# An encoder trunk on one core: both score matmuls of the attention over 128 rows, and the gate transposes of the mLSTM placed later in the program

## The chip, the cores and the metric

The kernel runs on one core of one Trainium2 chip. The metric is the device time of one execution in microseconds, as the median of repeated runs. A profile of one execution shows five engines: PE (TensorE: matmuls and transposes, with the loading of stationary operands as PEld), DVE (VectorE), ACT (ScalarE), POOL (GpSimd) and SP, whose queue issues the DMA transfers.

## The reference

Two layers on a sequence of 512 tokens with 1024 features. Each layer adds three normed sub-layers to the stream: a SwiGLU feed-forward, a mixer, a second SwiGLU feed-forward. The mixer projects its input once (`proj = h @ w_in`) and feeds two groups of heads:

- eight attention heads of 64 dimensions, with partial rotary on q and k, and three dilated windows whose outputs are merged by their softmax denominators. For the kernel this is one softmax over all 512 keys under a mask that holds the logarithm of how many windows contain a pair: `scores = q k^T + mask`, `out = softmax(scores) v`;
- four mLSTM heads of 128 dimensions in two directions, with input and forget gates (running sums and maxima of gate values along the sequence), whose sum is normed and gated.

Both are concatenated and sent through one output projection. All of it is in float32.

## The kernel before

**Exactness by halves.** PE multiplies in a float32 form that keeps fewer bits, so an operand is split into a high part (a rounding copy on ACT) and a low part (source minus high, on DVE, `lo` at line 114 and others), and a product is made of several matmuls into the same PSUM bank: `mm3` at lines 117 to 120 does high times high, high times low, low times high, each contracting over 128 rows.

**The scores.** A head has only 64 dimensions, so two parts fit into the 128 partitions. `stack` (lines 821 to 835) transposes the q or the k of a pair of heads (`hp`, two heads `e` = 0 and 1) into one PSUM bank, and reads it out. For k it puts the high part of a head on one half of the partitions of `ks[:, e]` and the low part on the other half. For q it puts the high part on both halves of `qh[:, e]`, and the low part of each head on that head's own half of `ql`, which has 512 columns for both heads. `scores(n)` (lines 848 to 865) then makes one tile of 128 queries by 512 keys of one head with two matmuls of 512 columns: line 855 contracts 128 rows (high q times high k plus high q times low k), line 856 contracts the 64 rows of the head's half (low q times high k). There are 32 such tiles in a layer, two layers, so 64 executions of each line. After them come the masked minimum on DVE (line 860), the exponential on ACT (862), a reciprocal on DVE, a scaling on POOL (864), four transposes on PE (871), and for every four tiles the value matmuls (887), `lead` = 2 tiles behind the scores.

The stacks are made at four places: for pair 0 in `opening` (line 642), for pairs 1 to 3 behind tiles 3, 13 and 17 (line 897). The banks of the four stacks are 5, 2, 2 and 7. The scores use banks 5 and 0 (later 5 and 4) in turn, so the first score tile uses the bank that stack 0 used.

**Buffers.** A tag with a number of buffers is handed from one user to the next in the order in which the program asks for tiles, and the first writer of a new user waits for the last reader of the old one. `ql` lies in the tags t0 and t1 (line 613). Tag "nt" has two buffers of 1024 columns: the normed rows of a token tile between sub-layers (`chain`, line 906), a weight tile of the feed-forward (329), and the `cell` of an mLSTM head (796), which the head's `mlstm_tail` writes with POOL and reads last with the four transposes of line 811. The tail of a head runs inside the main part of the next head, at its steps 1, 5 and 9; the tail of the fourth head runs at the end of `opening`.

**The mixer's order** (lines 523 to 658). First the value and output-gate projections in `groups` for tokens 0 to 255, the transposed q and k projections, and group 0 for the other tokens, after which `mixer_gates` makes the gates: DVE works out logarithms, PE turns them (689, 690), ACT copies, DVE scans and adds (700 to 708), then PE transposes 18 pieces of 8 rows (712), ACT copies them, PE reverses a part (717). Then groups 1 to 3 for the other tokens. After that `opening` runs the four heads step by step, and `paced` places pieces of the remaining projections between the steps: a piece is queued on PE behind an earlier step's last matmul (`issue_after`, issue order only). The rest of the attention is paced in the same way, first with the last projections, then with the first half of the output projection (`out_half`, lines 409 to 412).

The order on each engine's queue is set by a scheduler that takes the traced program in order of priority as operands become ready in its own simulation (`schedule_with_timeline_sim`, line 990). On the chip a queue is worked off in that order, and waits are for data alone.

Of the kernel before, what the change touches and what calls it, by code (L numbers as in the profile page):

```python
# [10 lines left out]
F32 = mybir.dt.float32  # L11
BF16 = mybir.dt.bfloat16
F32R = mybir.dt.float32r
# [5 lines left out]
P = 128  # L19
S = 512  # L20
NT = S // P
D = 1024
# [19 lines left out]
def trunk_kernel(ctx, tc, x, norm_gain, ffn_w_in, ffn_w_out, mix_w_in, conv_w, conv_b,  # L42
# [41 lines left out]
    def t2(name, slot, dt=F32):  # L84
        return tp.tile([P, 516], dt, tag=f"t{slot}", name=name, bufs=1)
# [55 lines left out]
    def last_ins(engine):  # L141
        return next(i for i in reversed(nc.cur_bb.bb.instructions) if i.engine == engine)
# [359 lines left out]
    def run(*gens):  # L502
        for g in gens:
            for _ in g:
                pass
# [17 lines left out]
    def mixer(layer, xx):  # L523
# [44 lines left out]
        qk = mixer_proj_T(layer, cvt, xx)  # L568
        run(proj_nat(layer, xx, *groups[0], tiles=(2, 3)))
        gates = mixer_gates(gt)  # L570
        for n, g in enumerate(groups[1:]):
            run(proj_nat(layer, xx, *g, tiles=(2, 3), per=1 + (n < 2)))

        def nat(name, slot):
            return [chunk(name, slot + q)[:, :1024].rearrange("p (t c) -> p t c", t=2) for q in range(2)]
# [34 lines left out]
        def stack_pair(hp):  # L610
            base = (20, 4)[hp % 2]
            ks, qh = pair("kst", base), pair("qsh", base + 1)
            ql = t2("qsl", hp % 2, F32R)[:, :512]
            stack(kn, hp, ks, None)
            stack(qn, hp, qh, ql)
            stacks[hp] = (ks, qh, ql)
# [43 lines left out]
    def mixer_gates(gt):  # L660
        g5 = gt.rearrange("p t (d y c) -> p t d y c", d=2, y=2)
        gi, gf = g5[:, :, :, 0, :], g5[:, :, :, 1, :]
        gs = chunk("gs", 20)
        cols = gs[:, :320].rearrange("p (t d c) -> p t d c", t=NT, d=2)
        G.memset(gs[:, :320], 0.0)

        def sv(q):
            return gs[:, 320 + q * 32: 352 + q * 32].rearrange("p (t d c) -> p t d c", t=NT, d=2)
        a, e, z, w, pl = [sv(q) for q in range(5)]
        V.scalar_tensor_tensor(a, gf, -1.0, gf, ALU.mult, ALU.max)  # L670
        A.activation(e, a, AF.Exp, scale=-1.0)
        V.tensor_scalar(z, e, 2.0, None, ALU.add)
        V.reciprocal(z, z)
        V.tensor_tensor(z, z, e, ALU.mult)
        V.tensor_tensor(w, z, z, ALU.mult)
        V.tensor_scalar(pl, w, 1.0 / 17.0, None, ALU.mult)
        for n in (15.0, 13.0, 11.0, 9.0, 7.0, 5.0, 3.0):
            V.scalar_tensor_tensor(pl, pl, 1.0 / n, w, ALU.add, ALU.mult)
        V.scalar_tensor_tensor(pl, pl, 1.0, z, ALU.add, ALU.mult)
        V.tensor_scalar(a, gf, 0.0, None, ALU.min)  # L680
        for d in range(2):
            V.scalar_tensor_tensor(cols[:, :, d, 4 * d: 4 * d + 4], pl[:, :, d], -2.0, a[:, :, d], ALU.mult, ALU.add)
            V.tensor_copy(cols[:, :, d, 32 + 4 * d: 36 + 4 * d], gi[:, :, d])
        g1, g2, g3, g4 = [chunk("gates", 15 + q)[0:8] for q in range(4)]
        lf, ig, fl = g3[:, 512:1024], g4[:, 0:512], g4[:, 512:1024]
        ps = psB("grow")
        for c in range(NT):
            o = ps[0:40, c * P: (c + 1) * P]
            PE.matmul(o, cols[:, c, 0, :], ident, start=True, stop=False)
            PE.matmul(o, cols[:, 3 - c, 1, :], rev, start=False, stop=True)  # L690
        A.copy(lf, ps[0:8, :])
        A.copy(ig, ps[32:40, :])
        on = ones[0:8].to_broadcast([8, P])
        fl4 = fl.rearrange("p (t c) -> p t c", t=NT)
        am = g1[:, :512].rearrange("p (t c) -> p t c", t=NT)
        mm = g1[:, 512:1024].rearrange("p (t c) -> p t c", t=NT)

        def bb(q):
            return g2[:, q * P: (q + 1) * P] if q < 8 else g3[:, (q - 8) * P: (q - 7) * P]
        V.tensor_tensor_scan(mm.rearrange("p t c -> p (t c)"), lf, ig, -BIG, ALU.add, ALU.max)  # L700
        for c in range(NT):
            V.tensor_tensor_scan(fl4[:, c], on, lf[:, c * P: (c + 1) * P], 0.0, ALU.mult, ALU.add)
        V.tensor_tensor(am, fl4, mm, ALU.subtract)
        V.tensor_tensor(g2[:, :512].rearrange("p (t c) -> p t c", t=NT), ig.rearrange("p (t c) -> p t c", t=NT), fl4, ALU.subtract)
        for d in range(1, 4):
            for i in range(4 - d):
                V.tensor_scalar(bb(bb_index(i, d)), bb(bb_index(i, d - 1)),
                                fl4[:, i + d - 1, P - 1: P], None, ALU.add)
        pn = psB("gnat")
        for q in range(18):  # L710
            row = g1[:, q * P: (q + 1) * P] if q < 8 else bb(q - 8)
            PE.transpose(pn[:, q * 8: q * 8 + 8], row, ident[0:8, 0:8])
        gn = one.tile([P, 216], F32, tag="gn", name="gn")
        n1 = gn[:, :144].rearrange("p (q c) -> p q c", c=8)
        A.copy(n1.rearrange("p q c -> p (q c)"), pn[:, :144])
        pj = psB("grev")
        PE.matmul(pj[:, :72], rev, n1[:, :, 4:8], start=True, stop=True)
        n2 = gn[:, 144:216].rearrange("p (q c) -> p q c", c=4)
        A.copy(n2.rearrange("p q c -> p (q c)"), pj[:, :72])
        em = one.tile([P, 4, NT, 2], F32, tag="gem", name="gem")  # L720
        for t in range(NT):
            A.activation(em[:, :, t, 0], n1[:, 4 + t, 0:4], AF.Exp, scale=-1.0)
            A.activation(em[:, :, t, 1], n2[:, 7 - t, :], AF.Exp, scale=-1.0)
        return n1, n2, em

    ps_abc, ps_st = banks_of(0), banks_of(1, 2)

    def mlstm_head(h, qk, gates, vx, smo, o):
        hold = {}
        return mlstm_main(h, qk, gates, vx, hold), mlstm_tail(h, gates[2], smo, o, hold)  # L730

    def mlstm_main(h, qk, gates, vx, hold):
# [54 lines left out]
    def mlstm_tail(h, em, smo, o, hold):  # L787
        hs = hold["hs"]
        den = small("den", 8).rearrange("p (t d) -> p t d", t=NT)
        dv = hs[:, :, :, 128]  # L790
        V.scalar_tensor_tensor(den, dv, -1.0, dv, ALU.mult, ALU.max)
        V.tensor_tensor(den, den, em[:, h], ALU.max)
        V.reciprocal(den, den)
        hv = hs[:, :, :, :128]
        G.tensor_tensor(hv, hv, den.unsqueeze(3).to_broadcast([P, NT, 2, P]), ALU.mult)
        nt = one.tile([P, D], F32, tag="nt", name="cell", bufs=2)
        cell, junk = [nt[:, q * 512: q * 512 + 512].rearrange("p (t c) -> p t c", t=NT) for q in range(2)]
        G.tensor_tensor(cell, hv[:, :, 0], hv[:, :, 1], ALU.add)
        yield
        ss = small("cell_ss", 4)  # L800
        G.tensor_tensor(junk, cell, cell, ALU.mult)
        V.tensor_reduce(out=ss, in_=junk, op=ALU.add, axis=mybir.AxisListType.X)
        r = rsqrt(ss, 4, 1.0 / P, EPS)
        G.tensor_tensor(cell, cell, r.unsqueeze(2).to_broadcast([P, NT, P]), ALU.mult)
        for q in range(2):
            cq = cell[:, 2 * q: 2 * q + 2]
            G.tensor_tensor(cq, cq, smo[q][:, :, h * P: (h + 1) * P], ALU.mult)
        yield
        ps = ps_po("ctr")
        for t in range(NT):  # L810
            PE.transpose(ps[:, t * P: (t + 1) * P], cell[:, t], ident)
        A.copy(o[:, 0], ps)
        V.tensor_tensor(o[:, 1], ps, o[:, 0].bitcast(F32), ALU.subtract)
        yield
# [6 lines left out]
    def stack(src, hp, dh, dl):  # L821
        ps = bank((5, 2, 2, 7)[hp], "stk")
        for t in range(NT):
            PE.transpose(ps[:, t * P: (t + 1) * P], src[t // 2][:, t % 2, hp * P: (hp + 1) * P], ident)
        lo, hi = slice(0, 64), slice(64, 128)
        if dl is None:
            A.copy(dh[lo, 0], ps[lo])
            V.tensor_tensor(dh[hi, 0], ps[lo], dh[lo, 0].bitcast(F32), ALU.subtract)
            A.copy(dh[hi, 1], ps[hi])
            V.tensor_tensor(dh[lo, 1], ps[hi], dh[hi, 1].bitcast(F32), ALU.subtract)  # L830
        else:
            for e, s, o in ((0, lo, hi), (1, hi, lo)):
                A.copy(dh[s, e], ps[s])
                A.copy(dh[o, e], ps[s])
                V.tensor_tensor(dl[s], ps[s], dh[s, e].bitcast(F32), ALU.subtract)

    def attention(stack_pair, stacks, pts, av, mask, mm):
        sms = {}
# [9 lines left out]
        def scores(n):  # L848
# [2 lines left out]
            t = half * 2 + u  # L851
            ps = bank((5, 0 if n < 16 else 4)[n % 2], "sc")
            c = slice(t * P, (t + 1) * P)
            hs = slice(e * HD, (e + 1) * HD)
            PE.matmul(ps, qh[:, e, c], ks[:, e], start=True, stop=False)
            PE.matmul(ps, ql[hs, c], ks[hs, e], start=False, stop=True)
            sm = t2("sm", 2 + n % 4)[:, :512]
            mx, dn = small("mx", 1, 4), small("dn", 1, 4)
            m0 = 384 - P * t
# [134 lines left out]
```

## Time and profile before

| | |
|---|---|
| median of 3 runs | 2132.06 us (2131.26 to 2143.67) |
| profiled execution, its own time | 2134.65 us |
| span of that execution on the core | 2132.9 us |
| PE busy | 2069.2 us, 97% of the span |
| PE loading weights | 1859.1 us, 87% |
| DVE, ACT, POOL busy | 1532.7, 1135.7, 313.4 us |
| mean granted TensorE clock | 0.992 of full speed |
| chain of waits, by engine | PE 84%, DVE 8%, DMA 3%, issue 3%, ACT 2% |

Times in the profile are microseconds unless marked ns. "Issue" is idle time for which the profile shows no wait. Matmuls are pipelined and the ends that the profile gives them are modelled, so the spacing of their starts says more than their durations. In a row, `out<-in` names the tiles, then come rows by columns of the stationary operand, rows by columns of the moving one, and the count; square brackets hold the idle time just before and what ended it. The attention of layer 0 lies between about 565 and 690 us of the span, that of layer 1 about 1052 us later.

### The profile page before, as it was taken

How to read it: one execution, taken by the hardware profiler on the slowest of the kernel's cores; microseconds unless marked ns; L12 is line 12 of the kernel's file. 1: busy time of each engine (PE TensorE's matmuls, PEld its weight loads, DVE VectorE, ACT ScalarE, POOL GpSimd, SP SyncE). 2: the span in 40 equal slices, each digit the busy share in tenths (PEclk: the TensorE clock that was granted, in tenths of full speed). 3: DMA queues.
4: the chain of work that ended last, by engine and by line, in shares of the span. 5: the costliest groups of instructions: out<-in, count | busy, mean ns of one | idle time of the engine just before them, and what ended most of it. 6: DMA issues, size and time to landing. Idle time of an engine off the chain costs nothing.

```text
span 2132.9 us, 35684 instructions
## 1 busy us (share of the span) xinstructions
PE 2069.2 (97%) x13918; PEld 1859.1 (87%) x13918; DVE 1532.7 (72%) x2572; ACT 1135.7 (53%) x2036; POOL 313.4 (15%) x358
## 2 busy tenths in 40 slices
PE   7999999999999999999999999999999999999998
PEld 6999988889976899998899999888898679999886
DVE  6688757785666878875787886667756568788665
ACT  5455546545565645555654555554455555455554
POOL 3000001433522300000030000014334122000000
PEclk9999999999999999999999999999999999999999
DMA  6533355541112653335565333554411236433364
GB/s 190 165 106 107 101 185 189 156 118 54 59 51 89 188 158 100 102 99 187 186 188 149 100 105 122 188 187 139 119 40 41 75 122 177 123 109 109 113 206 147
DMA packets 305887, 274.49 MB, mean 129 GB/s; under 512 B 8789, under 2 KB 275509, under 8 KB 305718
## 3 DMA queue, kind: packets, MB, share of 16 engines
q1 hardware_dynamic: 305718, 272.21, 42.5%
q8 instruction: 109, 1.79, 0.4%
q14 instruction: 60, 0.49, 0.1%
HBM read 270.08 MB, written 2.10 MB: 128 GB/s over the span
## 4 chain that ended last, share of the span: by engine, by line
PE 84%; DVE 8%; DMA 3%; issue 3%; ACT 2%; POOL 0%; SPq 0%; DVEq 0%; POOLq 0%; ACTq 0%
PE o L409 9%; PE o L412 9%; PE o L410 9%; PE pa L246 6%; PE pa L247 6%; PE pa L248 6%; PE pc L246 3%; PE pc L248 3%; PE pc L247 3%; PE nat L493 3%; PE nat L494 3%; PE nat L495 3%; PE po L887 2%; PE pb L247 1%; PE pb L248 1%
## 5 line engine op out<-in xcount | busy, mean ns | idle before, releaser
L114 DVE TENSOR_TENSOR lo<-raw,hi 128x1024 fp32r<-128x1024 f32 (+1 forms) x272 | 338.0, 1243 | 228.0 <-ACT hi L113 227.5
L113 ACT CAST hi<-raw 128x1024 fp32r<-128x1024 f32 (+1 forms) x280 | 294.7, 1053 | 321.9 <-PE o L412 226.9
L290 DVE TENSOR_TENSOR lo<-ws,hi 128x1024 fp32r<-128x1024 f32 x136 | 166.6, 1225 | 111.6 <-ACT hi L288 111.6
L410 PE MATMUL o<-lo,hq 128*128 128x512 f32 x704 | 236.9, 394 | 0.8 <-DVE lo L114 0.8
L412 PE MATMUL o<-hi,hq 128*128 128x512 f32 x704 | 223.3, 394 | 0.0
L409 PE MATMUL o<-hi,hq 128*128 128x512 f32 x704 | 210.5, 395 | 2.5 <-ACT hq L446 2.5
L288 ACT CAST hi<-ws 128x1024 fp32r<-128x1024 f32 x136 | 142.9, 1051 | 123.3 <-PE pc L247 114.8
L493 PE MATMUL nat<-hi,xh 128*128 128x256 f32 (+1 forms) x640 | 187.2, 294 | 0.0
L248 PE MATMUL gu<-xh,lo 128*128 128x256 f32 x640 | 181.7, 286 | 4.3 <-DVE lo L98 3.7
L494 PE MATMUL nat<-lo,xh 128*128 128x256 f32 (+1 forms) x640 | 182.7, 286 | 2.5 <-DVE lo L114 2.3
L247 PE MATMUL gu<-xl,hi 128*128 128x256 f32 x640 | 181.8, 285 | 2.7 <-DVE xl L201 2.7
L246 PE MATMUL gu<-xh,hi 128*128 128x256 f32 x640 | 182.0, 286 | 0.4 <-ACT hi L97 0.4
L495 PE MATMUL nat<-hi,xl 128*128 128x256 f32 (+1 forms) x640 | 182.3, 286 | 0.0
L246 PE MATMUL pa<-tq,hi 128*128 128x256 f32 x544 | 154.4, 284 | 14.5 <-ACT ha L353 14.5
L409 PEld LDWEIGHTS o<-hi,hq 128*128 128x128 f32 x704 | 131.9, 188 | 34.0 <-ACT hq L446 3.4
L246 PE MATMUL pc<-xh,hi 128*128 128x256 f32 x544 | 160.5, 295 | 0.0
L410 PEld LDWEIGHTS o<-lo,hq 128*128 128x128 f32 x704 | 131.9, 188 | 31.4 <-DVE lo L114 1.1
L412 PEld LDWEIGHTS o<-hi,hq 128*128 128x128 f32 x704 | 132.2, 188 | 30.8
L247 PE MATMUL pa<-tq,hi 128*128 128x256 f32 x544 | 154.4, 284 | 0.0
L248 PE MATMUL pa<-tq,lo 128*128 128x256 f32 x544 | 154.3, 284 | 0.0
L248 PE MATMUL pc<-xh,lo 128*128 128x256 f32 x544 | 153.7, 282 | 0.0
L247 PE MATMUL pc<-xl,hi 128*128 128x256 f32 x544 | 153.7, 282 | 0.0
(237 smaller groups left out, 5679.3 us busy)
## 6 DMA issues: line engine op xcount, KB each, us to landing
raw<-in_ffn_w_out_dram SPq DMA_DIRECT2D x176, 512.0 KB, 3.5
raw<-in_ffn_w_in_dram SPq DMA_DIRECT2D x146, 512.0 KB, 4.0
wu<-in_ffn_w_in_dram SPq DMA_DIRECT2D x68, 512.0 KB, 3.9
raw<-in_mix_w_in_dram SPq DMA_DIRECT2D x56, 512.0 KB, 3.8
raw<-in_mix_w_out_dram SPq DMA_DIRECT2D x32, 512.0 KB, 3.8
raw<-in_mix_w_in_dram SPq DMA_DIRECT2D x16, 528.0 KB, 3.8
gpost<-in_norm_gain_dram SPq DMA_DIRECT2D x6, 512.0 KB, 5.8
gpre<-in_norm_gain_dram SPq DMA_DIRECT2D x5, 512.0 KB
```

The lines of the kernel that those rows point to most:

```text
L113: A.copy(h, r)
L114: (sub or V).tensor_tensor(l, r, h.bitcast(F32), ALU.subtract)
L246: PE.matmul(ps, wh[:, k], xh[:, k], start=start and k == 0, stop=False, skip_group_check=True)
L247: PE.matmul(ps, wh[:, k], xl[:, k], start=False, stop=False, skip_group_check=True)
L248: PE.matmul(ps, wl[:, k], xh[:, k], start=False, stop=k == 3, skip_group_check=True)
L290: V.tensor_tensor(lo, src, fp(hi), ALU.subtract)
L409: PE.matmul(banks[t][n], a, wh[:, n], start=first, stop=False)
L410: PE.matmul(banks[t][n], a, wl[:, n], start=False, stop=False)
L412: PE.matmul(banks[t][n], b, wh[:, n], start=False, stop=end)
L493: PE.matmul(d, xh[:, k, tok], wh[:, k % 4], start=k == 0, stop=False)
L494: PE.matmul(d, xh[:, k, tok], wl[:, k % 4], start=False, stop=False)
L495: PE.matmul(d, xl[:, k, tok], wh[:, k % 4], start=False, stop=k == NK - 1)
```

## The change

Three things are edited. `ql` becomes a tile of two times 512 columns like `qh`, with the low part of each head on both partition halves, so that line 856 contracts all 128 rows (the added product is low q times low k); that takes four subtractions on DVE in a stack of q where there were two. The tile moves from the tags t0 and t1 to the tag "nt", and the `cell` tile of a head is asked for when the head is set up, ahead of its main part, and no longer in its tail. And `mixer_gates` becomes a generator in two parts: the first, through the scans and sums on DVE, runs at its old place, the second, from the 18 transposes on, is traced after group 2 and its PE instructions are queued behind group 2's last matmul.

```diff
--- before.py
+++ after.py
@@ -568,8 +568,12 @@
         qk = mixer_proj_T(layer, cvt, xx)
         run(proj_nat(layer, xx, *groups[0], tiles=(2, 3)))
         gates = mixer_gates(gt)
+        next(gates)
         for n, g in enumerate(groups[1:]):
             run(proj_nat(layer, xx, *g, tiles=(2, 3), per=1 + (n < 2)))
+            if n == 1:
+                with tc.issue_after(last_ins(mybir.EngineType.PE)):
+                    gates = next(gates)
 
         def nat(name, slot):
             return [chunk(name, slot + q)[:, :1024].rearrange("p (t c) -> p t c", t=2) for q in range(2)]
@@ -610,7 +614,7 @@
         def stack_pair(hp):
             base = (20, 4)[hp % 2]
             ks, qh = pair("kst", base), pair("qsh", base + 1)
-            ql = t2("qsl", hp % 2, F32R)[:, :512]
+            ql = one.tile([P, D], F32R, tag="nt", name="qsl", bufs=2).rearrange("p (a s) -> p a s", a=2)
             stack(kn, hp, ks, None)
             stack(qn, hp, qh, ql)
             stacks[hp] = (ks, qh, ql)
@@ -706,6 +710,7 @@
             for i in range(4 - d):
                 V.tensor_scalar(bb(bb_index(i, d)), bb(bb_index(i, d - 1)),
                                 fl4[:, i + d - 1, P - 1: P], None, ALU.add)
+        yield
         pn = psB("gnat")
         for q in range(18):
             row = g1[:, q * P: (q + 1) * P] if q < 8 else bb(q - 8)
@@ -721,12 +726,12 @@
         for t in range(NT):
             A.activation(em[:, :, t, 0], n1[:, 4 + t, 0:4], AF.Exp, scale=-1.0)
             A.activation(em[:, :, t, 1], n2[:, 7 - t, :], AF.Exp, scale=-1.0)
-        return n1, n2, em
+        yield n1, n2, em
 
     ps_abc, ps_st = banks_of(0), banks_of(1, 2)
 
     def mlstm_head(h, qk, gates, vx, smo, o):
-        hold = {}
+        hold = {"nt": one.tile([P, D], F32, tag="nt", name="cell", bufs=2)}
         return mlstm_main(h, qk, gates, vx, hold), mlstm_tail(h, gates[2], smo, o, hold)
 
     def mlstm_main(h, qk, gates, vx, hold):
@@ -793,7 +798,7 @@
         V.reciprocal(den, den)
         hv = hs[:, :, :, :128]
         G.tensor_tensor(hv, hv, den.unsqueeze(3).to_broadcast([P, NT, 2, P]), ALU.mult)
-        nt = one.tile([P, D], F32, tag="nt", name="cell", bufs=2)
+        nt = hold["nt"]
         cell, junk = [nt[:, q * 512: q * 512 + 512].rearrange("p (t c) -> p t c", t=NT) for q in range(2)]
         G.tensor_tensor(cell, hv[:, :, 0], hv[:, :, 1], ALU.add)
         yield
@@ -832,7 +837,8 @@
             for e, s, o in ((0, lo, hi), (1, hi, lo)):
                 A.copy(dh[s, e], ps[s])
                 A.copy(dh[o, e], ps[s])
-                V.tensor_tensor(dl[s], ps[s], dh[s, e].bitcast(F32), ALU.subtract)
+                V.tensor_tensor(dl[s, e], ps[s], dh[s, e].bitcast(F32), ALU.subtract)
+                V.tensor_tensor(dl[o, e], ps[s], dh[s, e].bitcast(F32), ALU.subtract)
 
     def attention(stack_pair, stacks, pts, av, mask, mm):
         sms = {}
@@ -851,9 +857,8 @@
             t = half * 2 + u
             ps = bank((5, 0 if n < 16 else 4)[n % 2], "sc")
             c = slice(t * P, (t + 1) * P)
-            hs = slice(e * HD, (e + 1) * HD)
             PE.matmul(ps, qh[:, e, c], ks[:, e], start=True, stop=False)
-            PE.matmul(ps, ql[hs, c], ks[hs, e], start=False, stop=True)
+            PE.matmul(ps, ql[:, e, c], ks[:, e], start=False, stop=True)
             sm = t2("sm", 2 + n % 4)[:, :512]
             mx, dn = small("mx", 1, 4), small("dn", 1, 4)
             m0 = 384 - P * t
```

## Rows read from the trace of the kernel before

**Rows 1.** The page's first part: busy time (share of span) xinstructions per engine.
```profile
PE 2069.2 (97%) x13918; PEld 1859.1 (87%) x13918; DVE 1532.7 (72%) x2572; ACT 1135.7 (53%) x2036; POOL 313.4 (15%) x358
```

**Rows 2.** Busy time by stretch: length, PE, PEld, DVE, ACT, POOL, PEclk, DMA share, GB/s.
```profile
478.00:492.00 14.00, 10.87 (x81) 9.53 (x79) 10.20 (x16) 5.27 (x16) 7.39 (x4) 0.89 0.45 129
600.00:640.00 40.00, 37.80 (x228) 27.44 (x227) 24.38 (x59) 25.41 (x51) 8.34 (x12) 1.00 0.23 67
640.00:680.00 40.00, 39.71 (x197) 25.31 (x197) 22.22 (x57) 20.09 (x42) 11.88 (x15) 1.00 0.28 92
```

**Rows 3.** Who PE waited for, whole span: us in total, times, longest.
```profile
PE gnat L712 <- DVE gates L707: 5.4, 4, 1.6
PE pt L871 <- ACT pts L876: 2.4, 4, 1.0
PE sc L855 <- ACT qsh L834: 2.0, 4, 0.8
```

**Rows 4.** Line 856 alone: duration ns min/median/max; then what ended idle time before it.
```profile
L856 PE MATMUL sc<-kst,qsl x64: 491/498/502, 566.0 to 1722.2; 64*128 64x512 f32 x64
...
  issue: 16.3, 58
```

**Rows 5.** Timeline of PE, one score tile among output-projection matmuls: start us, us, ...
```profile
649.72 0.40 PE L855 MATMUL sc<-kst,qsh 128*128 128x512 f32 x1
650.05 0.49 PE L856 MATMUL sc<-kst,qsl 64*128 64x512 f32 x1
650.47 0.50 PE L409 MATMUL o<-hi,mrg 128*128 128x512 f32 x1
650.80 0.40 PE L410 MATMUL o<-lo,mrg 128*128 128x512 f32 x1
```

**Rows 6.** Timeline of PE, an unbroken run of 128-row matmuls with 512 columns.
```profile
501.20 0.39 PE L118 MATMUL st<-qkp 128*128 128x512 f32 x1
...
501.90 0.39 PE L118 MATMUL st<-qkp 128*128 128x512 f32 x1
```

**Rows 7.** Timeline of DVE, PE, POOL and PE again, opening of attention, layer 0.
```profile
560.45 0.67 DVE L835 TENSOR_TENSOR qsl<-stk,qsh 64x512 fp32r<-64x512 f32 x1
...
565.21 0.39 PE L855 MATMUL sc<-kst,qsh 128*128 128x512 f32 x1
...
565.32 1.41 POOL L807 TENSOR_TENSOR cell<-cell,smo 128x256 f32<-128x256 f32 x2
...
570.09 0.38 PE L811 MATMUL ctr<-idj,cell 128*128 128x128 f32 x2
```

**Rows 8.** Timeline of PE and DVE, fourth cell's last transposes, second low part.
```profile
591.32 0.38 PE L811 MATMUL ctr<-idj,cell 128*128 128x128 f32 x2
...
595.13 0.68 DVE L835 TENSOR_TENSOR qsl<-stk,qsh 64x512 fp32r<-64x512 f32 x1 [1.00 <-ACT qsh L834]
```

**Rows 9.** Line 835 alone, laid out as rows 4; last, who waited for it.
```profile
L835 DVE TENSOR_TENSOR qsl<-stk,qsh x16: 672/689/695, 560.5 to 1692.5; 64x512 fp32r<-64x512 f32 x16
...
  ACT qsh L833: 4.8, 4
```

**Rows 10.** Timeline of DVE, ACT, fourth stack, layer 0.
```profile
637.77 0.68 DVE L835 TENSOR_TENSOR qsl<-stk,qsh 64x512 fp32r<-64x512 f32 x1 [1.83 <-ACT qsh L834]
...
638.49 0.58 ACT L833 CAST qsh<-stk 64x512 fp32r<-64x512 f32 x1
```

**Rows 11.** Timeline of PE around the gate transposes, layer 0.
```profile
475.93 0.28 PE L495 MATMUL nat<-hi,xl 128*128 128x256 f32 x1
...
485.59 1.30 PE L712 MATMUL gnat<-idj,gates 8*128 8x8 f32 x15
488.00 0.42 PE L712 MATMUL gnat<-idj,gates 8*128 8x8 f32 x2 [1.11 <-DVE gates L707]
490.01 0.27 PE L712 MATMUL gnat<-idj,gates 8*128 8x8 f32 x1 [1.59 <-DVE gates L707]
...
495.20 0.41 PE L493 MATMUL nat<-hi,xh 128*128 128x256 f32 x1
```

## The prediction, made before the changed kernel was run

> **What bounds the kernel now.** I read the engines' shares first: PE is busy 97% of the span and no other engine more than 72% [rows 1]. Time comes off only where PE's own work shrinks or where PE stands waiting. So next the waits of PE: beside the start of the program and the chains between sub-layers, which the change does not touch, they are 5.4 us before the gate transposes and 4.4 us in the attention, both layers together [rows 3]. That PE is busy does not say that it is at its peak, so third I looked at single lines that the diff touches. Line 856 stands out: its matmul takes 498 ns over 64 rows, and before its weights were loaded PE's loader stood 16.3 us in 58 of the 64 cases with no cause shown [rows 4]. The stretches of the attention show the cover for everything else: of 40 us there, DVE works 22 to 24 and ACT 20 to 25 [rows 2].
>
> **The first term: line 856 over 128 rows.** The price is read from starts, since ends are modelled. From the start of line 855 through line 856 and one matmul more to the start of a fourth, 650.80 - 649.72 = 1.08 us pass [rows 5]. Three matmuls of the same 512 columns, all over 128 rows, take 501.90 - 501.20 = 0.70 us [rows 6]. The excess is 0.38 us: 0.10 before line 856 starts, 0.19 until the next starts, 0.10 behind that one (0.33 where 0.23 is the rule). The one thing that sets line 856 apart in these rows is its 64 rows. So 64 x 0.38 = 24.3 us of PE time go. Lower bound: only the longer matmul itself, 498 against 390 ns [rows 4, 6], 64 x 0.108 = 6.9 us. Upper bound: the idle of the loader and the longer step behind it, 16.3 + 64 x 0.19 = 28.5 us [rows 4, 5]. A loss is excluded, since no 128-row matmul in these rows is spaced wider than 0.23 us among its like. I take 24.3, which rests on starts. The Trainium skill (TensorE: Matmul & The Clock Gate, section Why this matters for your kernels) says that a single matmul over few rows takes as long as one over 128, what is gained by few rows being that several can run at once. By that rule this term would be nothing; the spacing above speaks against it in this kernel, where a 64-row matmul stands alone among 128-row ones.
>
> **The second term: the low part moves into tag "nt".** The tag has two buffers, and the order of requests becomes cell 3, cell 4, `ql` 0, `ql` 1 and so on. So `ql` 0 takes the buffer of the third head's cell, and its writers wait for the last transposes of that cell. Now `ql` 0 is first written at 560.45, while those transposes run until 570.09 + 0.38 = 570.47 [rows 7]: a new wait, queued on DVE. How early can the cell be free? POOL is done with it at 565.32 + 1.41 = 566.73; four transposes at 0.38 a pair make it 567.49. Then the rest of the stack: DVE twice, ACT twice, DVE twice. That ACT waits for DVE there is seen in 4.8 us of waiting, and in a copy that starts at 638.49, right behind the subtraction from 637.77 to 638.45 [rows 9, 10]; both read the same bank. With 0.69 us for a subtraction and 0.58 for a copy, 4 x 0.69 + 2 x 0.58 = 3.92 us, so 571.4. The first score tile uses the same bank 5 as stack 0 and can start only then, not at 565.21: 6.2 us later. In these 6.2 us PE also has value matmuls, transposes and projection pieces that do not depend on it; what lacks are the two score tiles that ran there, 2 x (0.33 + 0.42) = 1.5 us [rows 5]. I take 2.0 us of standing per layer, 4.0 in all, since the pieces queued behind the second score tile shift too. Ends: nothing (other pieces fill it) and the whole 6.2 us, 12.4 in all. If PE stands that long the clock may fall as it did by the gates, where the granted clock was 0.89 over 14 us, worth 1.5 us [rows 2]: 3.0 more at the upper end.
>
> `ql` 1 takes the buffer of the fourth cell, whose transposes end at 591.32 + 0.38 = 591.70, and is written at 595.13 [rows 8]: 3.4 us of room. Eight score tiles ahead of it bring it forward by at most 3.0, so I cost this at nothing; without the room the writers would stand for what is missing. `ql` 2 and 3 follow score tiles that are done, as in the old tags, and the rows of the next sub-layer come only behind the value matmuls.
>
> **The third term: two more subtractions in a stack.** 16 x 0.69 = 11.0 us of DVE work [rows 9], covered by DVE's idle 40% in these stretches [rows 2]; without that cover it would come on top in full. But each stack's chain grows by 1.38 us before its bank is free. Stacks 1 and 2 are made some tiles ahead. The fourth one is not: around 634 to 640 PE already waits for ACT, (2.4 + 2.0) / 2 = 2.2 us a layer [rows 3], so there a shorter matmul only lengthens a wait. I take back the gain of four tiles, 4 x 0.38 = 1.5, and add 1.38: 2.9 a layer, 5.8 in all. Ends: nothing, and eight tiles and three stacks, 8 x 0.38 + 3 x 1.38 = 7.2 a layer, 14.4 in all.
>
> **The fourth term: the gate transposes.** The last 256-column matmul of group 2 starts at 475.93, the first gate transpose at 485.59 [rows 11]. In PE's queue the transposes already stand behind groups 1 and 2, so the new condition is met as things are, and their copies on ACT follow them. What PE waits for there is DVE's adds (1.11 and 1.59 us before the last three transposes), and DVE's part keeps its place. I cost it at nothing. Ends: if the order changes after all and other work covers the stall, 2.7 + 1.5 of clock = 4.2 us a layer gained, 8.4 in all [rows 2, 3]; the same lost, if the stall doubles.
>
> **The sum.** -24.3 + 4.0 + 5.8 + 0 = -14.5 us. Against the profiled execution, 2134.65, that is 2120.2; this execution lies 2.6 above the median of the runs, so the forecast of a median is 2132.06 - 14.5 = 2117.6, rounded to 2117.5. About 1% (21.3 us) is what a measurement of this kernel can tell from no change: the limits are 2110.7 and 2153.4.
>
> **The rivals.**
> - *Forecast*, 58%: most of the spacing comes back, part is lost at the opening and at stack 4. 2108 to 2127.
> - *Nothing is lost*, 10%: projection pieces fill the opening, stack 4 only shifts. -24.3, 2107.8. For it: PE's waits in the attention are small. Against: bank 5 ties the first score tile to the late `ql` 0.
> - *The gates gain too*, 8%: -14.5 - 8.4 = -22.9, 2109.2. Against: the condition is already met, so half of what the change says does nothing.
> - *The gain turns into waits*, 12%: behind the score come DVE, ACT, POOL and transposes, with two tiles of lead; if this chain sets the pace, PE only stands more. ACT is busy 25 of 40 us where PE is at its thinnest [rows 2], which speaks for it in that stretch only. -6 to +3, 2126 to 2135.
> - *Rows do not matter*, 4%: the excess has another cause than the 64 rows (that the two matmuls read the same keys one after the other, say), and the first term is nothing. +9.8, 2141.9. It is what the quoted rule of the Trainium skill would give.
> - *Slower by the opening*, 8%: the transposes of the third cell keep their place, ending at 570.47; the first score waits until 574.4, 9.2 us later than now, PE has nothing queued ahead of it, and the clock falls: (9.2 + 1.5) x 2 + 5.8 - 24.3 = +2.9, 2135.0. It decides the sign from (24.3 - 5.8) / 2 = 9.3 us of standing per layer on. Against: PE has pieces that wait for no score, as rows 7 show by the time between the first score and the cell's transposes.
>
> **The numbers.** 2117.5 is the forecast's time. The range 2105 to 2133 takes in the forecast, both better cases, and the waits and the opening for the most part; outside are the case of no effect of rows and the upper ends of the bounds. Faster by over 1%: the two better cases for the most part (15%) and the lower edge of the forecast (8%), 23%. Slower by over 1% needs some 20 us of standing per layer at the opening, or upper ends together: 4%. Within 1%: 73%.
>
> **What would show it.** First term: line 856 with 128 rows, 0.23 us from start to start, no idle of the loader before it. Second: the first line 835 behind the third cell's line 811, the first score at 570 or later, and a wait of PE for line 835 there. Third: 32 executions of line 835, ACT waiting longer for it, PE's waits in the attention above 4.4 us. Fourth: rows 11 again, with the same two waits. It is wrong if the spacing stays at 0.33 and 0.42, if PE stands over 9 us at an opening, or if the stall at the gates is gone.

## The result, and the profile after

The changed kernel takes 2115.5 us (median of 4 runs, 2109.14 to 2116.3), beside 2134.11 us for the kernel before in the same set: a ratio of 0.9899, 95% interval 0.9861 to 0.9936. That is 18.6 us less, where 14.5 less was forecast. The profiled execution took 2115.5 us, its span is 2113.8 where it was 2132.9.

The page's first part, as rows 1, says that the work shrank on PE: 21.7 us less busy in 19.1 us less span, with as many matmuls as before, and 16 instructions and 11 us more on DVE.

```profile
span 2113.8 us, 35704 instructions
PE 2047.5 (97%) x13918; PEld 1861.2 (88%) x13918; DVE 1544.0 (73%) x2588; ACT 1133.4 (54%) x2036; POOL 313.2 (15%) x358
```

Where it went is seen by the length of a stage: from the first score matmul (line 855, now 860) to the first matmul of the next feed-forward (`gu`, line 246). The two lines of each kernel in layer 0 (count, duration ns min/median/max, first and last start), first before, then after:

```profile
L855 PE MATMUL sc<-kst,qsh x32: 387/397/505, 565.2 to 669.8; 128*128 128x512 f32 x32
...
L246 PE MATMUL gu<-xh,hi x160: 277/280/384, 707.9 to 770.6; 128*128 128x256 f32 x160
```

```profile
L860 PE MATMUL sc<-kst,qsh x32: 387/396/504, 565.9 to 660.5; 128*128 128x512 f32 x32
...
L246 PE MATMUL gu<-xh,hi x160: 277/280/365, 698.3 to 761.0; 128*128 128x256 f32 x160
```

Before, the stage lasts 707.9 - 565.2 = 142.7 us, after, 698.3 - 565.9 = 132.4; in layer 1 it is 142.7 and 132.1. So 10.3 + 10.6 = 20.9 us come from these two stages, more than the whole difference. Of the two stages together PE is busy 280.3 us before and 258.5 after, 21.7 less, and idle 5.1 and 6.0. The first score itself starts 0.7 us later than before, and the gate transposes far ahead of it already start 1.4 us later in this execution (487.00, below, where rows 11 have 485.59).

The second score matmul, as rows 4. Its duration fell from 498 to 394 ns, and the idle of the loader with no cause shown is gone:

```profile
L861 PE MATMUL sc<-kst,qsl x64: 387/394/484, 567.5 to 1703.7; 128*128 128x512 f32 x64
```

A score tile among output-projection matmuls, as rows 5: five starts, 0.23, 0.24, 0.22 and 0.24 us apart, where they were 0.33, 0.42 and 0.33.

```profile
643.03 0.39 PE L860 MATMUL sc<-kst,qsh 128*128 128x512 f32 x1
643.26 0.40 PE L861 MATMUL sc<-kst,qsl 128*128 128x512 f32 x1
643.50 0.39 PE L410 MATMUL o<-lo,mrg 128*128 128x512 f32 x1
643.72 0.40 PE L409 MATMUL o<-hi,mrg 128*128 128x512 f32 x1
643.96 0.40 PE L410 MATMUL o<-lo,mrg 128*128 128x512 f32 x1
```

The opening, as rows 7, in the timeline of DVE, PE and POOL:

```profile
560.86 0.67 DVE L840 TENSOR_TENSOR qsl<-stk,qsh 64x512 fp32r<-64x512 f32 x1
561.55 0.68 DVE L841 TENSOR_TENSOR qsl<-stk,qsh 64x512 fp32r<-64x512 f32 x1
...
565.93 0.39 PE L860 MATMUL sc<-kst,qsh 128*128 128x512 f32 x1
...
570.85 0.38 PE L816 MATMUL ctr<-idj,cell 128*128 128x128 f32 x2
...
574.41 1.10 POOL L803 TENSOR_TENSOR cell<-hs 128x512 f32<-128x512 f32 x1
```

The low part of pair 0 is written at 560.86, ten microseconds before the third head's cell is read out. The wait that was forecast for it is not there. A wait fell to the fourth head's cell instead: on POOL's queue line 803 waits for a semaphore once, at 571.3, right behind the end of the transposes at 570.85 + 0.38 = 571.23:

```profile
L803 POOLq EVENT_SEMAPHORE  x1: 17/17/17, 571.3 to 571.3; - x1
```

That line ran at 573.1 before and runs at 574.4 now, with POOL at other work until then (lines 800 and 869), so the wait costs nothing that the profile shows.

PE's waits, as rows 3 (us in total, times, longest). The gates are unchanged. In the attention there are 2.9 + 2.6 + 0.5 = 6.0 us where there were 5.0 (2.4 and 2.0 in rows 3, and 0.6 for line 860, which the prediction left out), and one is new: the value matmuls, whose bank 7 is that of the fourth stack, wait for the added subtraction, line 841.

```profile
PE gnat L717 <- DVE gates L711: 5.4, 4, 1.6
PE pt L876 <- ACT pts L881: 2.9, 4, 0.9
PE po L892 <- DVE qsl L841: 2.6, 2, 1.3
PE sc L860 <- ACT qsh L839: 0.5, 2, 0.2
```

The gate transposes, as rows 11, with the same two waits to the hundredth:

```profile
487.00 1.30 PE L717 MATMUL gnat<-idj,gates 8*128 8x8 f32 x15
489.41 0.42 PE L717 MATMUL gnat<-idj,gates 8*128 8x8 f32 x2 [1.11 <-DVE gates L711]
491.42 0.22 PE L717 MATMUL gnat<-idj,gates 8*128 8x8 f32 x1 [1.59 <-DVE gates L711]
```

### The profile page after: what moved, and what is told of

Same layout as the page of the kernel before. It is cut to its first block, busy times and chain, and to the rows that moved or that the text cites. A ratio compares the mean times of both kernels' runs of the same rounds, so it can differ in the third digit from the quotient of the medians.

```text
span 2113.8 us, 35704 instructions
## 1 busy us (share of the span) xinstructions
PE 2047.5 (97%) x13918; PEld 1861.2 (88%) x13918; DVE 1544.0 (73%) x2588; ACT 1133.4 (54%) x2036; POOL 313.2 (15%) x358
## 4 chain that ended last, share of the span: by engine, by line
PE 84%; DVE 9%; issue 3%; ACT 2%; DMA 1%; POOL 0%; SPq 0%; DVEq 0%; POOLq 0%; ACTq 0%
PE o L409 9%; PE o L412 9%; PE o L410 9%; PE pa L246 6%; PE pa L247 6%; PE pa L248 6%; PE pc L246 3%; PE pc L248 3%; PE pc L247 3%; PE nat L493 2%; PE nat L494 2%; PE nat L495 2%; PE gu L247 2%; PE gu L248 2%; PE gu L246 2%
## 5 line engine op out<-in xcount | busy, mean ns | idle before, releaser
L412 PEld LDWEIGHTS o<-hi,hq 128*128 128x128 f32 x704 | 132.2, 188 | 30.8
```

The costliest lines, as they stand in the source:

```text
L412: PE.matmul(banks[t][n], b, wh[:, n], start=False, stop=end)
```

## The experiments

The theory: a 64-row matmul between 128-row ones costs PE 0.38 us a tile over a 128-row one, PE sets the pace of the attention, and nothing else in the change gains anything. Its rivals: the gain is that of the gates or of the new order of the queues; or the cost is each 64-row matmul's own, and not that of changing the rows. Eleven runs were made: eight edited kernels, one of them (e8) twice, and the changed kernel twice more. "Stage" is the length defined above, layer 0 and layer 1, in the profiled execution. In e7, e8 and e10 some projection matmuls run ahead of the stage, so their stages are not like the others'.

| kernel | median us | ratio to before (95%) | stage us |
|---|---|---|---|
| before | 2134.1 to 2135.7 | 1 | 142.7, 142.7 |
| changed | 2115.5 | 0.9899 (0.9861 to 0.9936) | 132.4, 132.1 |
| e2_gates_only | 2137.27 | 1.0008 (0.9995 to 1.002) | 142.7, 142.5 |
| e3_64_rows | 2130.44 | 0.9983 (0.9972 to 0.9995) | 141.3, 142.8 |
| e4_paired | 2114.84 | 0.9906 (0.9891 to 0.9922) | 133.4, 133.4 |
| e5_zeros | 2111.89 | 0.9896 (0.988 to 0.9912) | 132.1, 133.4 |
| after_again | 2113.09 | 0.9903 (0.9881 to 0.9925) | 133.9, 132.3 |
| e9_subs_twice | 2136.56 | 1.0007 (0.9992 to 1.0022) | 143.4, 141.4 |
| e7_fill | 2108.56 | 0.9888 (0.9862 to 0.9913) | 130.3, 131.5 |
| e8_zeros_fill | 2107.62 | 0.9866 (0.984 to 0.9893) | 130.4, 131.6 |
| after_third | 2112.2 | 0.9897 (0.9875 to 0.992) | 132.6, 132.2 |
| e8_again | 2105.0 | 0.9861 (0.9837 to 0.9885) | 130.4, 131.8 |
| e10_paired_fill | 2110.67 | 0.9892 (0.9871 to 0.9914) | 130.6, 130.6 |

The scheduler plans each kernel anew, so an edit also moves instructions that it does not name. In a diff of the built PE queues, by operation and tiles, 158 of some 13600 matmuls and transposes stand elsewhere in the changed kernel than before, 60 elsewhere in e3 than in the changed kernel, and 22 elsewhere in e5 than before.

**e2_gates_only**: the kernel before with the gate half of the diff alone.

> The kernel before with the gate half of the change alone. Theory A (the gate half does nothing, since the transposes already stood behind groups 1 and 2 in PE's queue): the same queues, so the time of before, within 0.3% (about 2134), and the same two waits of 1.1 and 1.6 us at the transposes. Rival (the gates gain too, as in the prediction's third case): up to 8 us less, 2126.

No difference: 1.0008, the stages as before. The order of the instructions on each of the five queues is the same, line for line, in the two built kernels; so it is between the changed kernel and one with its other half alone, which was not run for that reason. The gate half of this change does nothing.

**e3_64_rows**: the changed kernel with the rows undone.

```diff
-            PE.matmul(ps, ql[:, e, c], ks[:, e], start=False, stop=True)
+            hs = slice(e * HD, (e + 1) * HD)
+            PE.matmul(ps, ql[hs, e, c], ks[hs, e], start=False, stop=True)
```

> The changed kernel with one thing undone: the second score matmul contracts the 64 rows of the head's own half again; the four subtractions, the buffers and the gates stay as changed. Theory A (the 64 rows between 128-row matmuls cost 0.38 us of PE a tile, and PE sets the pace): the 24 us come back and the subtractions stay, so 2132 to 2142, at or above before, and the starts are spaced 0.33, 0.42, 0.33 again. Rival (the gain came from the new order of the queues or the buffers, rows do not matter): it stays at 2115.

The stages are nearly as long as before again, 141.3 and 142.8, and the starts are spaced as in rows 5 (timeline of PE). The time lies 1.6 us under the range of the theory.

```profile
623.32 0.39 PE L860 MATMUL sc<-kst,qsh 128*128 128x512 f32 x1
623.64 0.50 PE L862 MATMUL sc<-kst,qsl 64*128 64x512 f32 x1
624.07 0.50 PE L410 MATMUL o<-lo,mrg 128*128 128x512 f32 x1
624.41 0.40 PE L412 MATMUL o<-hi,mrg 128*128 128x512 f32 x1
```

So the number of rows is worth 141.3 + 142.8 - 132.4 - 132.1 = 19.6 us, of which some 1.5 is a low clock in e3's layer 1 (granted 0.91 from 1672 to 1692 us, with the same waits as in layer 0). The rest of the change, subtractions and buffers, costs nothing in e3's stages: layer 0 is even 1.4 us shorter than before. PE's busy time is that of before to the tenth, 2069.2 us, and its waits in the attention are only these (rows as rows 3), 1.6 us against the 6.0 of the changed kernel:

```profile
PE pt L877 <- ACT pts L882: 1.1, 4, 0.4
PE po L893 <- DVE qsl L841: 0.5, 2, 0.2
```

The median lies 4.4 us under the 2134.85 of before; the stages give 285.4 - 284.1 = 1.3 of that. In the profiled executions the two spans differ by 2132.9 - 2127.6 = 5.3 us, and the first score alone comes 5.4 us earlier (559.8, where 565.2 before), behind a stretch that the edit leaves alone (last section).

**e4_paired**: the kernel before, with the order of the score matmuls changed.

```diff
-            PE.matmul(ps, qh[:, e, c], ks[:, e], start=True, stop=False)
-            PE.matmul(ps, ql[hs, c], ks[hs, e], start=False, stop=True)
+            if n % 2 == 0:
+                first(n)
+                first(n + 1)
+                with tc.issue_after(last_ins(mybir.EngineType.PE)):
+                    for m in (n, n + 1):
...
+                        PE.matmul(firsts[m], ql[hs, c], ks[hs, e], start=False, stop=True)
```

> The kernel before with the two second score matmuls of a pair of heads queued behind both first ones, so that two 64-row matmuls, on different halves of the partitions, follow one another; still 64 rows and two subtractions. Theory A1 (what costs is going from 128 rows to 64 and back): one such change for two tiles, so 32 x 0.38 = 12 us less, and 32 x 0.23 = 7 us more if the two run side by side, less what the later start of the even tile's softmax costs: 2113 to 2125. Theory A2 (each 64-row matmul costs 0.1 to 0.2 us by itself, whatever stands beside it): no gain from pairing, 2130 to 2138.

2114.84, as good as the changed kernel, with 64 rows. In the timeline of PE the two second matmuls are one row of 0.49 us, and the next matmul starts 0.42 us after them, as it does behind one alone. The group's row says the same: 64 of 495 ns in 17.0 us of busy time, 0.53 us for two, so they run in twos, side by side on the two halves.

```profile
602.03 0.39 PE L856 MATMUL sc<-kst,qsh 128*128 128x512 f32 x1
602.35 0.49 PE L870 MATMUL sc<-kst,qsl 64*128 64x512 f32 x2
602.77 0.39 PE L494 MATMUL nat<-lo,xh 128*128 128x256 f32 x1
602.99 0.28 PE L495 MATMUL nat<-hi,xl 128*128 128x256 f32 x1
...
L870 PE MATMUL sc<-kst,qsl 64*128 64x512 f32 x64 | 17.0, 495 | 0.0
```

For two tiles the excess is paid once: 0.09 us ahead, 0.42 for the pair, 0.10 behind (0.22 to the next start, where these matmuls of 256 columns lie 0.12 apart), 0.61 us in all, where two 128-row matmuls take 0.46 and two lone 64-row ones took 1.22. 32 x 0.61 = 19.5 us would be gained by that; the stages are 18.6 shorter than before. So what stands ahead and behind belongs to going from 128 rows to 64 and back. Whether the 0.19 by which a 64-row matmul holds up the next start belongs to that change too, or to each such matmul with the two running at the same time, this run does not separate. The step behind is not peculiar to rows: in the changed kernel the first 128-column matmul behind the value matmuls, whose stationary operand has 64 columns, is followed 0.34 us later, too (637.51 - 637.17; timeline of PE):

```profile
635.29 1.95 PE L892 MATMUL po<-pts,av 128*64 128x256 f32 x16 [1.28 <-DVE qsl L841]
637.17 0.50 PE L409 MATMUL o<-hi,mrg 128*128 128x512 f32 x1
637.51 0.39 PE L410 MATMUL o<-lo,mrg 128*128 128x512 f32 x1
```

The Trainium skill (TensorEngine Tiling (Array Packing), section Key Properties) states that changing the tiling mode drains the engine, while different tiles of one mode work in parallel. The trace agrees with both, as far as starts can show it, and adds the price. The rule of the Trainium skill that the prediction quotes, that a single matmul over few rows takes as long as one over 128, does not hold for a lone 64-row matmul among 128-row ones: e3 decides against it.

**e5_zeros**: the changed kernel with two of the four subtractions replaced by fills on POOL.

```diff
+            G.memset(ql[0:64, 1].bitcast(F32), 0.0)
+            G.memset(ql[64:128, 0].bitcast(F32), 0.0)
...
-                V.tensor_tensor(dl[o, e], ps[s], dh[s, e].bitcast(F32), ALU.subtract)
```

> The changed kernel with the other half of each low part set to zero by POOL instead of a second subtraction on DVE: two subtractions a stack again, still 128 rows (the product low times low is zero, as before the change). Theory A (the added subtractions lengthen the chain of each stack by 1.38 us, above all of the fourth): 2 to 6 us less than the changed kernel, 2109 to 2113, and PE's wait for line 841 at the value matmuls gone. Rival (that chain is covered): the same as the changed kernel, 2115, or slightly more if POOL's fills come late.

Its ratio, 0.9896, is that of the changed kernel, and its stages, 132.1 and 133.4, are not shorter, as the rival had it, though the median lies in the range of theory A, too. The wait at the value matmuls is gone, as theory A had it. Others stand in its place, 3.5 + 2.4 + 0.6 = 6.5 us in the attention:

```profile
PE pt L877 <- ACT pts L882: 3.5, 4, 1.5
PE sc L861 <- ACT qsh L841: 2.4, 4, 0.8
PE sc L861 <- DVE mx L866: 0.6, 2, 0.3
```

These are the waits of before, in nearly the queue of before, and not those of the changed kernel. So no time shows for the added subtractions, but e5 does not measure them by themselves. It is a second test of the rows: with the order nearly kept and two subtractions in both, its stages are 285.4 - 265.5 = 19.9 us shorter than before, with 1.5 us more of waits.

**after_again** and **after_third**: the changed kernel, as the measure for the sets that follow.

> The changed kernel once more, as the measure for the others of this set. Theory: 2113 to 2117, its attention stages (first score matmul to first matmul of the next feed-forward) 132 us where before has 142.7.

> The changed kernel a third time, as the measure for the next two. Theory: 2112 to 2116.

Both as expected. The stage varies from 132.1 to 133.9 us between executions of one kernel, with the same waits; in the longest the granted clock is 0.91 from 620 to 640 us, around the fourth stack, and 1.00 in the rest.

**e9_subs_twice**: the changed kernel with every subtraction of a stack of q done twice.

```diff
+                for w in (s, o):
+                    V.tensor_tensor(dl[w, e], ps[s], dh[s, e].bitcast(F32), ALU.subtract)
```

> The changed kernel with the two subtractions of each half of a stack of q done twice, four more a stack: the suspected cost of the third term doubled and more (2.8 us longer chain a stack, 22 us more work on DVE in all). Theory A (the longer chain of a stack is covered but for a wait of 1.3 us a layer at the value matmuls behind the fourth stack): that wait grows to about 4 us a layer, so 4 to 8 us more than the changed kernel, 2119 to 2124. Rival 1 (all of it covered): the same, 2115. Rival 2 (each stack pays): 16 x 1.4 = 22 us more, 2137.

23 us over the changed kernel, all that it had gained: the time of rival 2, but not by each stack paying. PE's waits for the subtractions (line 843) are 4.3 + 3.5 = 7.8 us, 3.9 a layer, as theory A had it; what theory A lacked is other waits and the clock. In layer 0 PE's waits in the attention sum to 8.8 us, where the changed kernel has 3.0, and 7.3 of them lie between 620 and 641 us, around the fourth stack; these are the longest, in the timeline of PE (start and duration in us, idle time just before in brackets):

```profile
626.41 0.63 PE L878 MATMUL pt<-idj,sm 128*128 128x128 f32 x4 [1.99 <-ACT pts L883]
...
634.63 0.79 PE L863 MATMUL sc<-kst,qsl 128*128 128x512 f32 x1 [2.13 <-DVE qsl L843]
...
639.42 3.68 PE L894 MATMUL po<-pts,av 128*64 128x256 f32 x16 [1.87 <-DVE qsl L843]
```

and the granted clock falls around them, to 0.50 (its lower level, 1.2 GHz) in the second of these stretches and 0.54 in the third, where the changed kernel has 1.00 (busy time by stretch, columns as rows 2, first e9, then the changed kernel):

```profile
630.00:635.00 5.00, 2.27 (x10) 1.25 (x8) 3.33 (x5) 2.08 (x4) 0.00 (x0) 0.84 0.01 3
635.00:640.00 5.00, 2.71 (x8) 1.18 (x9) 3.64 (x7) 1.59 (x4) 0.70 (x1) 0.50 0.00 0
640.00:645.00 5.00, 5.00 (x21) 2.94 (x18) 0.42 (x1) 0.38 (x1) 0.00 (x0) 0.54 0.00 0
```

```profile
630.00:635.00 5.00, 3.19 (x16) 1.75 (x14) 3.82 (x7) 2.65 (x6) 0.29 (x1) 1.00 0.27 102
635.00:640.00 5.00, 4.71 (x29) 3.35 (x30) 1.62 (x6) 1.46 (x3) 0.69 (x1) 1.00 0.00 0
640.00:645.00 5.00, 5.00 (x32) 3.43 (x31) 3.98 (x8) 3.19 (x7) 1.36 (x2) 1.00 0.45 124
```

In e9 the chain of the fourth stack then runs into a low clock, which lengthens it again (the sixteen value matmuls of line 894 take 3.68 us there, 1.95 in the changed kernel). Of the 143.4 - 132.4 = 11.0 us by which the stage of layer 0 grows, 5.8 are waits and 5.0 longer work of PE (busy 134.4 us, where 129.4). So no cost shows for the first two added subtractions, and the next four cost 9 to 11 us a layer (141.4 - 132.1 in layer 1): the cover at the fourth stack ends between them. The queue of e9 differs from the changed kernel's as well; what of the waits is due to that was not separated.

**e7_fill**: the changed kernel with three pieces of the projections ahead of the heads.

```diff
         proj = projections()
-        paced(opening(), 67, take(proj, 32), 32, 1)
+        for _ in range(3):
+            next(proj)
+        paced(opening(), 67, take(proj, 29), 29, 1)
```

> The changed kernel with three pieces of the projections (36 matmuls of 256 columns, 4.2 us) free to run before the first head, where all of them were queued behind the first head's first transposes. Theory A (PE stands at the gate transposes because nothing else may run there, 2.7 us a layer and some clock behind it): the two waits of 1.1 and 1.6 us go, 6 to 10 us less than the changed kernel, 2105 to 2110. Rival (the pieces compete with the gates on DVE and ACT, or PE runs dry later for lack of pieces): no change, 2115, with a new wait in the heads.

2108.56, 4.5 us under the changed kernel of its set, less than the 6 to 10 expected, and with overlapping intervals. The waits at the gates are gone, and part of what they gave is spent on new waits, in the first head and in the attention, where all waits sum to 8.5 us for the 6.0 of the changed kernel. That fewer pieces are left to run beside is the likely reason, not shown:

```profile
PE st L118 <- DVE wt L779: 3.2, 2, 1.6
PE pt L878 <- POOL sm L871: 4.3, 2, 2.1
```

**e8_zeros_fill** and **e8_again**: the edits of e5 and e7 together.

> Both: zeros on the other half of each low part (two subtractions a stack) and the three pieces ahead of the heads. Theory A: what the pieces give, and the wait at the value matmuls gone, 2.6 us in all: 2103 to 2108. Rival (subtractions covered): the same as the pieces alone.

> Zeros on the other half and three pieces ahead of the heads, once more beside the changed kernel, whose intervals touched in the last set. Theory: 4 to 8 us below the changed kernel, 2106 to 2110. Rival (the difference was that of single executions): the same, 2114.

2107.62 and 2105.0, ratios 0.9866 and 0.9861: by the medians 5.5 and 7.2 us under the changed kernel of the same set, and in the first set 0.9 under e7, which does not tell it from the pieces alone. Its gate stretch, as the first of rows 2, is full and at full clock (e8_again):

```profile
478.00:492.00 14.00, 13.94 (x109) 12.52 (x109) 10.27 (x16) 4.54 (x11) 7.39 (x4) 1.00 0.43 131
```

It beats the kernel before clearly. Against the changed kernel the intervals of either set overlap a little; that two sets agree makes a gain of some 6 us likely.

**e10_paired_fill**: the pairs of e4 with the pieces of e7.

> 64 rows with the second matmuls of a pair of heads side by side, two subtractions a stack, and the three pieces ahead of the heads. Theory (the two ways to avoid the changes of rows are worth about the same, and the pieces add the same 4 to 8 us): 2106 to 2112. Rival (the later softmax of the even tile uses up the cover at the fourth stack): 2115 or more.

2110.67, and 2105.0 for e8 in the same set: pairing gives no more than filling the rows. A fair stretch for the kernels with pieces runs from the first gate transpose to the next feed-forward, with 1406 matmuls in each kernel: 222.3 and 222.8 us before (layer 0, layer 1), 211.3 and 212.1 in the changed kernel, 210.7 and 211.9 in e7, 208.5 and 210.0 in e8_again, 209.6 and 209.7 in e10. So e10 lacks 0.8 us there; the rest of the difference lies outside and was not followed.

## Why the prediction was right, and which terms were not

*First term*, 24.3 us: right in mechanism, a little too large. e3 shows the rows to be the cause, and e5, in nearly the queue of before, agrees: 19.6 and 19.9 us of stage. PE's busy time falls by 21.7 us, from 2069.2, before and in e3 alike, to 2047.5. That is 0.34 us a tile; the 0.38 was read at one tile.

*Second term*, 4.0 us: wrong, it is nothing; none of its signs came, neither a first score at 570 nor a wait of PE for the low part there. The step that failed is "`ql` 0 takes the buffer of the third head's cell", which rested on buffers being handed out in the order of requests. The addresses in the built kernel show the third and the fourth cell in one buffer, the second cell, `ql` 0 and `ql` 1 in the other: the buffers went round in the order of first writes, and `ql` 0 is first written ahead of the fourth cell, though asked for behind it. No experiment forced the other order, so the slower rival, which hung on this wait, was not tried.

*Third term*, 5.8 us: right in place (the fourth stack, where the value matmuls now wait for line 841, 1.3 us a layer), too large against before: PE's waits in the attention grew from 5.0 to 6.0 us. Against e3 they grew by 4.4, but e3 has other waits than before with the same 64 rows, 1.6 us for 5.0, so the order of the queue, which differs too, can move them as much as the edit. Of its two reasons, that shorter matmuls lengthen PE's waits is borne out by e5 against before, by 1.5 us. That the two added subtractions lengthen them is open: the new wait is for one of them, but e5, which takes them away, has as much waiting elsewhere. Twice as many more cost far more than the 1.38 us a stack of the upper end: in e9 waits add up around the fourth stack, the granted clock falls, and the whole gain is gone.

*Fourth term*, nothing: right, and settled by e2: the stall at the gates stays, as rows 11 show it.

So the forecast had 24.3 - 9.8 = 14.5 us, and the stages show 21.7 of PE's work less 0.8 of added idle time, 20.9. The gain was put 2.6 too high and what is lost 9.0 too high; the one error hides part of the other, and outside the stages the execution lost some 2 us again. That the time came so near is in part luck. The time came 2.0 us under the forecast, and the ratio of 0.9899 lies on the line of 1%, below which the prediction had put 23% of the chance.

## What to carry to other kernels

Here a matmul over 64 rows between 128-row ones cost 0.34 to 0.38 us more than one over 128: look for it in the spacing of starts, and either fill the rows (with a second copy or with zeros) or put two such matmuls on different halves next to each other. Before costing a queueing edge, look whether the queue already has that order; what held PE at the gates was that all other work was queued behind them, and letting three pieces go first took the stall away. When an edit is compared, compare the built queues too: two kernels with the same 64 rows had 5.0 and 1.6 us of waits in two orders. Cover has an edge: a chain that showed no cost when it grew by 1.4 us cost some ten microseconds a layer at three times that, as three waits of some 2 us came within 13 us and the granted clock fell.

## What the runs showed that was not expected

The granted clock fell at waits of only some 2 us. In e9 the three longest, of 2.0, 2.1 and 1.9 us, end at 626.4, 634.6 and 639.4 us. The clock falls to 0.50 behind the first of them already, is back at 1.00 after 632 us, and falls again behind the second (columns as rows 2; for the stretches from 635 us on see e9):

```profile
626.00:628.00 2.00, 1.58 (x8) 1.39 (x9) 1.71 (x4) 0.98 (x3) 0.94 (x2) 0.89 0.48 111
628.00:630.00 2.00, 2.00 (x9) 1.70 (x8) 0.00 (x0) 0.06 (x1) 0.42 (x1) 0.50 0.37 152
632.00:634.00 2.00, 0.50 (x4) 0.26 (x3) 1.94 (x4) 0.00 (x0) 0.00 (x0) 1.00 0.03 8
```

At the gates, with waits of 1.11 and 1.59 us between transposes over 8 rows [rows 11], it was 0.89 over 14 us [rows 2].

The start of the kernel is not the same from one execution to the next. The kernel before stands 3.09 us at 44.5 us, waiting for a DVE subtraction of the first weights, and runs at the lower clock behind it; the profiled execution of e3 has no such wait there and reaches its first score 5.4 us earlier. First the row of before, then the stretch from 40 to 80 us of before and of e3 (columns as rows 2):

```profile
44.54 0.38 PE L248 MATMUL gu<-xh,lo 128*128 128x256 f32 x1 [3.09 <-DVE lo L98]
...
40.00:80.00 40.00, 36.91 (x297) 36.55 (x296) 26.84 (x33) 17.91 (x25) 4.90 (x2) 0.96 0.68 188
```

```profile
40.00:80.00 40.00, 40.00 (x340) 40.00 (x339) 27.65 (x31) 19.81 (x26) 4.10 (x2) 1.00 0.78 218
```

It is not the edit: of three profiled executions of the changed kernel two have that wait (3.09 and 2.99 us) and one has not, and their first gate transposes start at 487.0, 488.0 and 481.0 us. So single executions move by 6 to 7 us, more than some of the effects here, which is why stages were compared. What sets it was not looked into.
